# A hybrid attention and recurrent block: x loaded transposed, the norm applied to the products of ten weight chunks, h rescaled in place later

## The chip, the cores and the metric

One core of one Trainium2 chip runs the kernel. The metric is the device time of one execution in microseconds, the median of three runs. The engines are PE (matrix products), DVE (vector), ACT (activations, table functions), POOL (a second, general vector engine) and SP, which issues most of the DMAs.

## What is computed

One layer of a decoder block on x of 1024 tokens by 1024 features, float32. Cut to what the change is about:

```python
def rms_norm(x, g):
    y = x * rsqrt(mean(x * x, -1) + EPS)
    return y * g

h = rms_norm(x, norm_gain)
proj = h @ w_in
q, kv_all, g_nsa, br_gate, u_lru, g_lru, merge_g = split(proj)
y_a = nsa_mixer(q, kv_all, br_gate, ...)   # compressed, selected and window attention
y_a = (y_a * silu(g_nsa)) @ w_proj_a
y_b = rglru_mixer(u_lru, conv_w, ...)      # causal convolution, two gates, a scan over the tokens
y_b = (y_b * silu(g_lru)) @ w_proj_b
m = sigmoid(gate_a) * y_a + sigmoid(gate_b) * y_b
x = x + m @ w_out
```

There are 8 query heads of 64 in two groups with keys and values of their own, and the recurrent mixer is 512 wide.

## The kernel before

Tokens and features both lie in blocks of 128, and the tokens in two halves of 512. Each large product is made of float32 operands that are split in a high and a low part: `mm3` issues high by high (line 170), high by low (171) and low by high (172), so that all large products have these three lines. Weights are split as they come (`wsplit`, line 182 and on): the high part on ACT (line 184), the low part on POOL or DVE (line 185). h itself is needed transposed, features on partitions: `hT_h` (the tile is named big_h) and `hT_l` (big_l, one tile for each half).

**Head** (lines 195 to 239). x comes by eight token blocks of 512 KB (lines 217, 221), in between the first two weight chunks (`wload`, line 176) and the small parameters. For each block ACT squares and sums (line 228), POOL takes the power -1/2 (lines 192, 193), DVE multiplies the block by it (line 231). PE transposes each half by 32 blocks of 128x128 (line 235), four into a bank of PSUM; ACT copies the bank times the gain (line 237) and DVE makes the low part of it (line 238).

**Chunks.** `chunk(c)` (line 259) multiplies 128 columns of w_in with h: 24 products for each half of the tokens, in a bank of its own. Five banks take turns (`ps_5`: four named ps_s, one ps_f). Chunks 0 to 7 are u and the gate of the four parts of the recurrent mixer (`lru(n)`, line 321): ACT copies u out of the banks (line 325), DVE makes the convolution (330, 333), ACT and DVE split the result (336, 337), the silu of the gate is a sigmoid on ACT (343) and a product with the bank on DVE (344). After two small products ACT makes the two gates; DVE follows with lines 361, 362 (a RECIPROCAL of 128x1024), 363, 364, 366 and the scan 367, with POOL's products at 365 and 368. Chunks 8 and 9 are the compressed keys and values (`compress`, line 372). These parts are generators, and the string ORD, "0c1c0c2c1c323", says in which order they are taken a step further.

**q, k, v.** `qkv(g)` (line 469) projects q, the keys, values and branch gates for one group, with tokens on partitions, from block 7 down to block 0: 48 products of 262 columns into two banks for each block, copied by ACT (498, 499) and for the gates by DVE (500). Blocks 7 to 4 read the second half of h, 3 to 0 the first. For group 0 each block goes through `prep` at once: squares on ACT (531), sums (533), power on POOL (192, 193), products on DVE (536) and POOL (537, 538), split on ACT and DVE (541 to 546) and POOL (550), transposes (554, 561) and copies (556, 565). For group 1 the projection runs beside the scores of group 0. The tile named t has nine buffers, and st four.

The order on each engine is fixed when the program is built: a scheduler places the instructions by priorities and by durations of its own, and each engine then runs its list in order, waiting on semaphores.

Of the kernel before, what the change touches and what calls it, by code (L numbers as in the profile page):

```python
# [9 lines left out]
FT = mybir.dt.float32  # L10
# [16 lines left out]
SMALL = (("gain", 8), ("kgain", 192), ("qgain", 64), ("w4", 128), ("lru_p", 32), ("cb1", 4), ("pe", 32))  # L27
# [10 lines left out]
SO = (1, 1)  # L38
# [15 lines left out]
XW = 5  # L54
# [32 lines left out]
def _build(ctx, tc, A, out, dbg):  # L87
# [58 lines left out]
    # after the attention: banks and blocks that it held  # L146
# [32 lines left out]
    def wsplit(raw, k, into=None, E=None):  # L179
        """hi and lo parts of 1024 weights per partition, as [128, k, n]"""  # L180
# [18 lines left out]
    make_identity(nc, ident)  # L199
    G.tensor_copy(ident_r, ident)  # L200
    ident = f(ident_r)
    small = K.tile([128, NSMALL], FT, name="small")
    part = {}
# [4 lines left out]
    gain = part["gain"]  # L208
# [10 lines left out]
    dma(small, A["small"])  # L219
    for tb in range(4, 8):  # L220
        dma(xt[tb], A["x"][tb * 128:(tb + 1) * 128, :])
        if tb == XW:
            first.append(wload(A["w_in"][1]))
    for half in range(2):
        xs = xt[half * 4:half * 4 + 4]
        for b in range(4):
            tb = half * 4 + b
            C.activation(junk[:, (b % 2) * S:(b % 2 + 1) * S], xs[b], AF.Square, scale=DM ** -0.5,
                         accum_out=ssq[:, tb:tb + 1])
            rsq(rstd[:, tb:tb + 1], ssq[:, tb:tb + 1], EPS, 128, 1)  # L230
# [22 lines left out]
    def chunk_half(o, wh, wl, half):  # L253
        """o [128, 512] = w^T h^T, tokens of one half"""
# [4 lines left out]
    def chunk(c):  # L259
        E = EN[(CE >> c) & 1]  # L260
        wh, wl = wsplit(first.pop(0), 8, None, E) if first else wtile(A["w_in"][c], 8, None, E)
        s = []
# [36 lines left out]
    # -4 softplus(-lambda): log1p by the series of atanh  # L299
# [19 lines left out]
    yb = DR.tile([4, 128, S], FT, name="yb")  # L319

    def lru(n):
        s = chunk(2 * n)
# [15 lines left out]
        s = chunk(2 * n + 1)  # L338
# [15 lines left out]
        # t = tanh(log_a / 2): a = (1 + t) / (1 - t), sqrt(1 - a^2) = 2 sqrt(-t) / (1 - t)  # L354
# [18 lines left out]
    def compress():  # L373
        big, dup = p_slc(), p_win()
        kv = [big[:, j * S:(j + 1) * S] for j in range(2)]
        for j in range(2):
            s = chunk(8 + j)
            for half in range(2):
                C.activation(kv[j][:, half * 512:(half + 1) * 512], s[half], AF.Copy)
        yield  # L380
        for j in range(2):
# [3 lines left out]
            for g in range(2):  # L385
# [3 lines left out]
                for b in range(2):  # L389
                    # token 16 (c + b) + 2 l  # L390
# [716 lines left out]
```

## Time and profile before

| quantity | value |
|---|---|
| median of the runs (lowest, highest) | 909.04 us (908.88, 909.33) |
| profiled execution: span, device time | 908.0 us, 909.0 us |
| PE busy | 874.2 us, 96% of the span |
| DVE, ACT, POOL busy | 573.3, 439.1, 300.6 us |
| first product of a chunk on PE | at 15.81 us |
| first scores | at 239.90 us |

Times in the trace are microseconds from the start of the span. The busy time of an engine contains what an instruction stands still once it has begun; idle time is shown with the event that ended it. A busy PE is not always at its full clock: the granted clock stands in the windows.

### The profile page before, as it was taken

Reading aid. Unit: us, or ns where it says so; the run is one execution under the profiler, and the core shown is the slowest. Engines: PE = TensorE matmul, PEld = TensorE weight load, DVE = VectorE, ACT = ScalarE, POOL = GpSimd, SP = SyncE. Lnnn points to the kernel's source line nnn. Section 1 sums busy time; section 2 is a strip of 40 time slices with the busy share of each in tenths; the row PEclk is TensorE's granted clock in tenths of the full one; section 3 lists DMA queues with packets and bytes.
Section 4 is the critical chain, followed back from the end, with each engine's and each line's share of the span. In section 5 each row is a group of like instructions: output and inputs, shape, how many; then the busy total and the mean of one; then the engine's idle time right before and its main releaser. Section 6 shows DMA issues by size and latency. Waiting matters only on the chain.

```text
span 908.0 us, 15833 instructions
## 1 busy us (share of the span) xinstructions
PE 874.2 (96%) x5670; PEld 781.0 (86%) x5670; DVE 573.3 (63%) x1626; ACT 439.1 (48%) x1159; POOL 300.6 (33%) x339
## 2 busy tenths in 40 slices
PE   4999999989899999999999999999999899999998
PEld 3678878889899999999999998999999877888887
DVE  5642778897722447475687867677777886784111
ACT  6421434645523548575566666566667663321000
POOL 4122233169622325252455553243233421000000
PEclk9999999999999999999999999999999999999999
DMA  9215321121312112122121232111113469983111
GB/s 340 64 49 139 131 95 55 55 82 48 117 48 82 59 48 74 52 86 69 55 66 65 77 102 75 47 54 60 46 42 119 132 202 331 336 270 119 70 70 47
DMA packets 45519, 92.49 MB, mean 102 GB/s; under 512 B 6896, under 2 KB 12704, under 8 KB 45440
## 3 DMA queue, kind: packets, MB, share of 16 engines
q1 hardware_dynamic: 44480, 88.33, 28.9%
q0 software_dynamic: 960, 3.15, 0.9%
q8 instruction: 44, 0.72, 0.3%
q14 instruction: 35, 0.29, 0.1%
HBM read 64.15 MB, written 25.21 MB: 98 GB/s over the span
## 4 chain that ended last, share of the span: by engine, by line
PE 80%; DVE 7%; DMA 4%; POOL 4%; issue 2%; ACT 2%; SPq 0%; DVEq 0%; ACTq 0%; POOLq 0%
PE ps_f L170 9%; PE ps_f L171 9%; PE ps_f L172 9%; PE ps_s L612 7%; PE ps_s L170 7%; PE ps_s L171 7%; PE ps_s L172 7%; PE ps_t L665 6%; PE ps_t L170 4%; PE ps_t L171 4%; PE ps_t L172 4%; PE ps_o L690 3%; PE ps_o L689 3%; POOL ss L193 1%; DVE sq L536 1%
## 5 line engine op out<-in xcount | busy, mean ns | idle before, releaser
L171 PE MATMUL ps_f<-big_l,w_hi 128*128 128x256 f32 (+1 forms) x700 | 200.3, 286 | 0.0
L170 PE MATMUL ps_f<-big_h,w_hi 128*128 128x256 f32 (+1 forms) x664 | 193.8, 292 | 1.0 <-ACT ev L829 0.8
L172 PE MATMUL ps_f<-big_h,w_lo 128*128 128x256 f32 (+1 forms) x664 | 189.4, 285 | 0.0
L171 PEld LDWEIGHTS ps_f<-big_l,w_hi 128*128 128x128 f32 x700 | 131.9, 188 | 2.1
L170 PEld LDWEIGHTS ps_f<-big_h,w_hi 128*128 128x128 f32 x664 | 125.6, 189 | 4.1 <-ACT ev L829 2.3
L172 PEld LDWEIGHTS ps_f<-big_h,w_lo 128*128 128x128 f32 x664 | 125.4, 189 | 1.6
L670 DVE TENSOR_TENSOR pl<-ps_t,ph 128x512 fp32r<-128x512 f32 x132 | 90.4, 686 | 47.5 <-ACT ph L669 46.0
L185 POOL TENSOR_TENSOR w_lo<-w_raw,w_hi 128x1024 fp32r<-128x1024 f32 x33 | 80.7, 2448 | 102.1 <-ACT w_hi L184 101.7
L669 ACT ACTIVATE ph<-ps_t 128x512 fp32r<-128x512 f32 x132 | 78.1, 599 | 48.8 <-PE ps_t L665 45.6
L650 POOL TENSOR_SCALAR p_slc<-p_slc,mx,bg 128x384 f32<-128x384 f32 (+7 forms) x88 | 68.7, 786 | 89.5 <-DVE mx L649 34.8
L646 ACT ACTIVATE p_slc<-ps_s,mx 128x256 f32<-128x256 f32 (+5 forms) x128 | 68.1, 541 | 24.1 <-DVE mx L644 18.6
L171 PE MATMUL ps_s<-big_l,w_hi 128*128 128x512 f32 (+1 forms) x184 | 73.8, 401 | 0.0
L184 ACT ACTIVATE w_hi<-w_raw 128x1024 fp32r<-128x1024 f32 (+1 forms) x40 | 42.4, 1062 | 43.6 <-PE ps_f L171 17.5
L636 DVE TENSOR_REDUCE mx<-ps_s 128x1 f32<-128x256 f32 (+5 forms) x120 | 50.9, 436 | 11.0 <-PE ps_s L612 9.3
L170 PE MATMUL ps_s<-big_h,w_hi 128*128 128x512 f32 x136 | 55.3, 408 | 2.5 <-ACT big_h L237 2.5
L689 PE MATMUL ps_o<-ph,t 128*128 128x512 f32 x132 | 55.7, 422 | 0.0
L650 POOL TENSOR_SCALAR p_win<-p_win,mx,bg 128x640 f32<-128x640 f32 (+1 forms) x40 | 34.7, 869 | 59.3 <-DVE mx L649 25.5
L665 PE MATMUL ps_t<-ident_r,p_slc 128*128 128x128 f32 x336 | 54.2, 273 | 0.0
L612 PE MATMUL ps_s<-kTs,t 128*128 128x512 f32 (+4 forms) x224 | 53.0, 349 | 0.6 <-ACT pc L621 0.3
L172 PE MATMUL ps_s<-big_h,w_lo 128*128 128x512 f32 x136 | 53.5, 397 | 0.0
L641 DVE CUSTOM_DVE_ANT_0 ps_s<-ps_s,bias 128x256 f32<-128x256 f32 (+1 forms) x128 | 52.5, 417 | 1.4 <-PE ps_s L612 0.3
L690 PE MATMUL ps_o<-pl,t 128*128 128x512 f32 x132 | 53.2, 403 | 0.0
(331 smaller groups left out, 2213.3 us busy)
## 6 DMA issues: line engine op xcount, KB each, us to landing
w_raw<-in_w_in SPq DMA_DIRECT2D x30, 512.0 KB
t<-in_x SPq DMA_DIRECT2D x8, 512.0 KB
gb<-ev SPq DMA_DIRECT2D x16, 256.0 KB
ga<-ev SPq DMA_DIRECT2D x16, 256.0 KB
w_raw<-in_w_out SPq DMA_DIRECT2D x8, 512.0 KB
st<-mb SPq DMA_DIRECT2D x16, 256.0 KB
w_raw<-in_w_tok SPq DMA_DIRECT2D x6, 524.0 KB
ev<-in_cw SPq DMA_DIRECT2D x8, 256.0 KB
```

Of the source, the lines that this page charges most:

```text
L170: T.matmul(o, lh, rh, start=first, stop=False)
L171: T.matmul(o, lh, rl, start=False, stop=False)
L172: T.matmul(o, ll, rh, start=False, stop=last)
L185: (E or (V if tail else G)).tensor_tensor(out=lo, in0=raw, in1=f(hi), op=OP.subtract)
L612: T.matmul(s, qT[h][:, i * 128:(i + 1) * 128], rhs, start=(hl == 0), stop=(hl == 1))
L646: C.activation(p[:, h, k0:k1], sv, AF.Exp, bias=mx[:, 6:7], accum_out=mx[:, 7 + j:8 + j])
L650: G.tensor_scalar(out=p[:, h], in0=p[:, h], scalar1=mx[:, 9:10], scalar2=bg[:, g, i, 4 * (br + 1) + h:4 * (br + 1) + h + 1], op0=OP.mult, ...
L665: ins = T.transpose(pt[:, h * 128:(h + 1) * 128], p[h][:, c0:c0 + 128], ident)
L669: C.activation(ph, pt, AF.Copy)
L670: V.tensor_tensor(out=pl, in0=pt, in1=f(ph), op=OP.subtract)
L689: T.matmul(o, vf, pp[0], start=first, stop=False)
L690: T.matmul(o, vf, pp[1], start=False, stop=False)
```

## The change

- x comes in a second, transposed layout as well: eight tiles of 512 KB, features on partitions, four for each half of the tokens; the first one as two DMAs. The first weights come right behind it, the second behind the first half of x, the small parameters behind all of x, and the gain by a DMA of its own on ACT's queue.
- `split_x` makes h without the norm: gain times x on ACT, its low part on DVE. No transposes, no norm ahead of the products.
- `norms` makes the squares (ACT), their sums over tiles (DVE for the first half, POOL for the second), eight products of one column with ones that sum over partitions, the power on POOL, a diagonal on DVE, and one product of ones and the diagonal, which puts the norm of each token on all partitions: R, one tile of 128x512 for each half, in two of the four buffers of st.
- `chunks` takes two chunks together: both weights are held, the first half of the tokens for both, then the second. u, the gate and the compressed keys and values are multiplied by R as DVE reads them out of PSUM; the last product of the silu goes to POOL.
- `rescale(half)` turns h into the normed h in place: four times the sum of both parts on POOL, its product with R on DVE, the high part on ACT, the low part on DVE, each 128x1024. In the code the first half stands ahead of block 7 of group 0, the second ahead of block 3. Blocks 7 to 4 of group 0 still read the h without norm and are multiplied at the copy out of PSUM.

The core of the diff (lines with comments alone and the constants that are no longer used are left out):

```diff
-    xt = [ta() for _ in range(NT)]
-    for tb in range(4):
-        dma(xt[tb], A["x"][tb * 128:(tb + 1) * 128, :])
-    first = [wload(A["w_in"][0])]
...
-            rsq(rstd[:, tb:tb + 1], ssq[:, tb:tb + 1], EPS, 128, 1)
-            V.tensor_scalar(out=xs[b], in0=xs[b], scalar1=rstd[:, tb:tb + 1], scalar2=None, op0=OP.mult)
-        for kc in range(8):
-            pt = (ps_t, ps_t, ps_o)[SO[half] and kc % 3]()
-            for b in range(4):
-                T.transpose(pt[:, b * 128:(b + 1) * 128], xs[b][:, kc * 128:(kc + 1) * 128], ident)
...
+    R = [t_st() for _ in range(2)]
+    def split_x(half):
+        for j in range(4):
+            for k in range(2):
+                kc = 2 * j + k
+                hh = hT_h[:, kc, half * 512:(half + 1) * 512]
+                C.activation(hh, xt[half][j][:, k], AF.Copy, scale=gain[:, kc:kc + 1])
+                V.scalar_tensor_tensor(out=hT_l[half][:, kc], in0=xt[half][j][:, k],
+                                       scalar=gain[:, kc:kc + 1], in1=f(hh), op0=OP.mult, op1=OP.subtract)
+    def norms(half):
+        acc = junk[:, half * S:(half + 1) * S].rearrange("p (k n) -> p k n", k=2)
+        C.activation(acc, xt[half][0], AF.Square, scale=DM ** -0.5)
+        for j in range(1, 4):
+            C.activation(xt[half][j], xt[half][j], AF.Square, scale=DM ** -0.5)
+            (V, G)[half].tensor_tensor(out=acc, in0=acc, in1=xt[half][j], op=OP.add)
...
+                T.matmul(o[:, b:b + 1], acc[:, k, b * 128:(b + 1) * 128], ones[:, 0:1], start=(k == 0), stop=(k == 1))
...
+        T.matmul(o, ones, dg, start=True, stop=True)
+        V.tensor_copy(R[half], o)
+    split_x(0)
+    pending = [lambda: norms(0), lambda: split_x(1), lambda: norms(1)]
+    def rescale(half):
+        for j in range(4):
+            t = ta().rearrange("p (k n) -> p k n", k=2)
+            hh = hT_h[:, 2 * j:2 * j + 2, half * 512:(half + 1) * 512]
+            ll = hT_l[half][:, 2 * j:2 * j + 2]
+            G.tensor_tensor(out=t, in0=f(hh), in1=f(ll), op=OP.add)
+            V.tensor_tensor(out=t, in0=t, in1=R[half][:, None, :].to_broadcast([128, 2, 512]), op=OP.mult)
+            C.activation(hh, t, AF.Copy)
+            V.tensor_tensor(out=ll, in0=t, in1=f(hh), op=OP.subtract)
...
+        for half in range(2):
+            for k, (wh, wl) in enumerate(ws):
+                s[k][half] = ps_5()
+                chunk_half(s[k][half], wh, wl, half)
...
-            C.activation(u[:, half * 512:(half + 1) * 512], s[half], AF.Copy)
+            V.tensor_tensor(out=u[:, half * 512:(half + 1) * 512], in0=s[half], in1=R[half], op=OP.mult)
...
-            C.activation(sg[:, t], s[half], AF.Sigmoid)
-            V.tensor_tensor(out=sg[:, t], in0=sg[:, t], in1=s[half], op=OP.mult)
+            V.tensor_tensor(out=i[:, t], in0=sz[half], in1=R[half], op=OP.mult)
+            C.activation(sg[:, t], i[:, t], AF.Sigmoid)
+            G.tensor_tensor(out=sg[:, t], in0=sg[:, t], in1=i[:, t], op=OP.mult)
...
+        if not g:
+            rescale(0)
         for tb in range(NT - 1, -1, -1):
+            if not g and tb == 3:
+                rescale(1)
...
+                r = rstd[:, tb:tb + 1] if not g and tb > 3 else 1.0
+                C.activation(e[:, 0:262], o[0][:, 0:262], AF.Copy, scale=r)
+                C.activation(e[:, 262:512], o[1][:, 0:250], AF.Copy, scale=r)
+                V.tensor_scalar(out=bg[:, g, tb], in0=o[1][:, 250:262], scalar1=r, scalar2=None, op0=OP.mult)
```

Three places of the order that the prediction speaks of. In the changed kernel the lines of `mm3` are 168 to 170, 268 to 274 are `rescale`, and big_l_100 and big_l_101 are the low parts of the first and of the second half of h.

PE, the head, before: L235 are the transposes of x, L170 to L172 the products of the first chunk.

```order
L235 MATMUL ps_o<-ident_r,t 128x128
L235 MATMUL ps_t<-ident_r,t 128x128 [waits DVE_49]
L235 MATMUL ps_t<-ident_r,t 128x128
L235 MATMUL ps_o<-ident_r,t 128x128
L170 MATMUL ps_s<-big_h,w_hi 128x512 [waits Activation_49]
L235 MATMUL ps_t<-ident_r,t 128x128 [waits DVE_49]
L235 MATMUL ps_t<-ident_r,t 128x128 x3
L171 MATMUL ps_s<-big_l_75,w_hi 128x512
L172 MATMUL ps_s<-big_h,w_lo 128x512 [waits Pool_49]
L170 MATMUL ps_s<-big_h,w_hi 128x512 [waits Activation_49]
```

And now, from the first instruction on:

```order
L168 MATMUL ps_s<-big_h,w_hi 128x512 [waits Activation_49]
L169 MATMUL ps_s<-big_l_100,w_hi 128x512 [waits DVE_49]
L170 MATMUL ps_s<-big_h,w_lo 128x512 [waits DVE_49]
L168 MATMUL ps_s<-big_h,w_hi 128x512
L169 MATMUL ps_s<-big_l_100,w_hi 128x512
L170 MATMUL ps_s<-big_h,w_lo 128x512
```

The transposes are gone; the products wait for ACT's and DVE's parts of x alone.

DVE, between the branch gates of the first blocks of q, k, v and the last part of the recurrent mixer, before: L362, L363, L364, L366 and L367 are the mixer's RECIPROCAL, products and scan, L455 and L460 copies of a bias, L533 and L536 steps of `prep`.

```order
L362 RECIPROCAL t<-t 128x1024 [waits DVE_49]
L367 SCALAR_TENSOR_TENSOR t<-t,kTs 128x1024 [waits DVE_49]
L455 COPY bias<-t 128x1024 [waits DMAHW1_49,PE_49]
L536 TENSOR_TENSOR sq<-ev,ss 128x384 [waits Pool_49]
L455 COPY bias<-t 128x1024 [waits DMAHW2_49]
L500 COPY bg<-ps_s 128x12 [waits Activation_49]
L533 TENSOR_REDUCE ss<-sq 128x6 [waits Activation_49]
L460 COPY cbias<-t 128x512 [waits DMAHW4_49,DMAHW5_49,DMAHW3_49,DMAHW6_49,DMAHW2_49,DMAHW7_49,DMAHW1_49,DMAHW0_49]
L500 COPY bg<-ps_f 128x12 [waits Activation_49]
L363 SCALAR_TENSOR_TENSOR t<-t 128x1024 [waits DVE_49]
L364 SCALAR_TENSOR_TENSOR t<-t 128x1024
L344 TENSOR_TENSOR kTs<-kTs,ps_s 128x512 [waits Activation_49] x2
```

And now, at the place behind the same RECIPROCAL; L406, L407 and L410 are two products and the scan of the mixer, L272 and L274 the product and the subtraction of `rescale`, L580 to L593 steps of `prep`.

```order
L406 SCALAR_TENSOR_TENSOR t<-t 128x1024 [waits DVE_49]
L407 SCALAR_TENSOR_TENSOR t<-t 128x1024
L410 SCALAR_TENSOR_TENSOR t<-t,kTs 128x1024 [waits DVE_49]
L272 TENSOR_TENSOR t<-t,st 128x1024 [waits Pool_49]
L589 TENSOR_TENSOR st<-sq,st 128x4x64 [waits Activation_49]
L593 TENSOR_TENSOR st<-sq,st 128x2x128 [waits Activation_49]
L272 TENSOR_TENSOR t<-t,st 128x1024 [waits Pool_49] x2
L274 TENSOR_TENSOR big_l_100<-t,big_h 128x1024 [waits Activation_49]
L580 TENSOR_REDUCE ss<-sq 128x6 [waits Activation_49]
L272 TENSOR_TENSOR t<-t,st 128x1024 [waits Pool_49]
L274 TENSOR_TENSOR big_l_100<-t,big_h 128x1024 [waits Activation_49]
L583 TENSOR_TENSOR sq<-ev,ss 128x384 [waits Pool_49]
```

The rescaling stands behind the scan, and in between the preparation of the first blocks; each L272 waits for POOL's sum.

PE, the end of the fourth and the start of the fifth block of q, k, v (the first that reads the first half of h), before; p_slc and w_hi, w_lo hold the weights' parts:

```order
L171 MATMUL ps_s<-p_slc,big_h 128x262
L172 MATMUL ps_s<-p_slc,big_l_76 128x262
L170 MATMUL ps_f<-w_hi,big_h 128x262 [waits DVE_49]
L171 MATMUL ps_f<-w_lo,big_h 128x262
L172 MATMUL ps_f<-w_hi,big_l_75 128x262
```

And now:

```order
L169 MATMUL ps_s<-p_slc,big_h 128x262
L170 MATMUL ps_s<-p_slc,big_l_101 128x262
L168 MATMUL ps_f<-w_hi,big_h 128x262 [waits Activation_49]
L169 MATMUL ps_f<-w_lo,big_h 128x262
L170 MATMUL ps_f<-w_hi,big_l_100 128x262 [waits DVE_49]
```

Before, the block waited for a bank alone; now its products wait for ACT's and DVE's parts of the rescaled h.

## Rows read from the trace of the kernel before

**Rows 1.** The page: span; busy time of each engine, its share, instructions.
```profile
span 908.0 us, 15833 instructions
...
PE 874.2 (96%) x5670; PEld 781.0 (86%) x5670; DVE 573.3 (63%) x1626; ACT 439.1 (48%) x1159; POOL 300.6 (33%) x339
```

**Rows 2.** Windows: length; busy us (instructions) by engine; TensorE clock; DMA share; GB/s.
```profile
10.00:20.00 10.00, 6.00 (x20) 4.27 (x21) 8.70 (x21) 6.55 (x13) 5.46 (x8) 1.00 1.03 385
...
96.00:168.00 72.00, 71.45 (x383) 59.14 (x381) 56.04 (x43) 32.07 (x47) 22.30 (x12) 1.00 0.27 91
...
177.30:239.90 62.60, 55.81 (x441) 54.27 (x439) 55.32 (x76) 32.15 (x89) 48.59 (x52) 0.97 0.23 73
```

**Rows 3.** Waits of PE, 0 to 300 us: total us, times, longest us.
```profile
PE ps_t L235 <- DVE t L231: 9.7, 4, 7.3
...
PE ps_s L612 <- ACT t L565: 2.4, 1, 2.4
```

**Rows 4.** Timeline of PE, first 40 us: start, length, engine, line, operation [idle before].
```profile
15.81 0.80 PE L170 MATMUL ps_s<-big_h,w_hi 128*128 128x512 f32 x1 [2.50 <-ACT big_h L237]
...
31.92 0.47 PE L170 MATMUL ps_s<-big_h,w_hi 128*128 128x512 f32 x1
32.24 0.40 PE L171 MATMUL ps_s<-big_l,w_hi 128*128 128x512 f32 x1
32.47 0.39 PE L172 MATMUL ps_s<-big_h,w_lo 128*128 128x512 f32 x1
...
35.25 0.60 PE L235 MATMUL ps_t<-ident_r,t 128*128 128x128 f32 x4
35.60 0.48 PE L171 MATMUL ps_s<-big_l,w_hi 128*128 128x512 f32 x1
...
37.38 1.02 PE L280 MATMUL ps_o<-t,rel 32*8 32x512 f32 x2
38.33 0.50 PE L170 MATMUL ps_s<-big_h,w_hi 128*128 128x512 f32 x1
```

**Rows 5.** Timeline of ACT, first 12 us.
```profile
4.33 1.06 ACT L228 ACTIVATE p_win<-t 128x1024 f32<-128x1024 f32 x1 [2.31 <-DMA t<-in_x]
...
8.03 1.06 ACT L228 ACTIVATE p_win<-t 128x1024 f32<-128x1024 f32 x1 [1.31 <-DMA t<-in_x]
...
10.54 1.06 ACT L184 ACTIVATE w_hi<-w_raw 128x1024 fp32r<-128x1024 f32 x1
```

**Rows 6.** Lines of DVE by form, 168 to 240 us: busy us, mean ns.
```profile
L344 DVE TENSOR_TENSOR kTs<-kTs,ps_s 128x512 f32<-128x512 f32 x2 | 1.3, 674 | 0.0
```

**Rows 7.** Timeline of DVE, 168 to 240 us.
```profile
177.36 2.70 DVE L363 SCALAR_TENSOR_TENSOR t<-t 128x1024 f32<-128x1024 f32 x1
179.98 1.22 DVE L364 SCALAR_TENSOR_TENSOR t<-t 128x1024 f32<-128x1024 f32 x1
...
183.39 6.54 DVE L362 RECIPROCAL t<-t 128x1024 f32<-128x1024 f32 x1
...
201.09 2.54 DVE L542 TENSOR_TENSOR st<-sq,st 128x256 fp32r<-128x256 f32 x1
...
220.81 0.43 DVE L542 TENSOR_TENSOR st<-sq,st 128x256 fp32r<-128x256 f32 x1 [0.94 <-ACT st L541]
```

**Rows 8.** Timeline of POOL, 168 to 240 us.
```profile
176.54 2.44 POOL L365 TENSOR_TENSOR kTs<-kTs,t 128x1024 f32<-128x1024 f32 x1 [19.34 <-ACT kTs L352]
...
200.94 2.41 POOL L365 TENSOR_TENSOR kTs<-kTs,t 128x1024 f32<-128x1024 f32 x1
...
220.71 1.32 POOL L193 TENSOR_TENSOR ss<-ss,nhalf 128x6 f32<-128x6 f32 x1
```

**Rows 9.** Timeline of PE, 190 to 202 us.
```profile
196.15 0.39 PE L170 MATMUL ps_s<-w_hi,big_h 128*128 128x262 f32 x1 [2.80 <-DVE bg L500]
...
197.41 0.42 PE L170 MATMUL ps_s<-w_hi,big_h 128*128 128x262 f32 x1
...
200.68 0.30 PE L170 MATMUL ps_f<-w_hi,big_h 128*128 128x262 f32 x1
```

More of the change, by code (lines that the diff above doesn't have):

```diff
@@ L26 @@
 NB = 71
-SMALL = (("gain", 8), ("kgain", 192), ("qgain", 64), ("w4", 128), ("lru_p", 32), ("cb1", 4), ("pe", 32))
+SMALL = (("kgain", 192), ("qgain", 64), ("w4", 128), ("lru_p", 32), ("cb1", 4), ("pe", 32))
 NSMALL = sum(w for _, w in SMALL)
@@ L53 @@
 NPL = 3
-XW = 5
 PF = 1
@@ L198, in _build @@
     ident = junk[:, 2 * S:2 * S + 128]
-    make_identity(nc, ident)
-    G.tensor_copy(ident_r, ident)
-    ident = f(ident_r)
+    ones = junk[:, 2 * S + 128:2 * S + 256]
+    gain = K.tile([128, 8], FT, name="gain")
+    nc.scalar.dma_start(gain, A["gain"])
+    xt = [[ta().rearrange("p (k n) -> p k n", k=2) for _ in range(4)] for _ in range(2)]
+    first = []
+    for half in range(2):
+        for j in range(4):
+            if (half, j) == (0, 0):
+                for k in range(2):
+                    dma(xt[0][0][:, k], A["xT"][0, 0, :, k])
+                first.append(wload(A["w_in"][0]))
+            else:
+                dma(xt[half][j], A["xT"][half, j])
+            if (half, j) == (0, 3):
+                first.append(wload(A["w_in"][1]))
     small = K.tile([128, NSMALL], FT, name="small")
+    dma(small, A["small"])
     part = {}
@@ L207, in _build @@
         c0 += w
-    gain = part["gain"]
+    make_identity(nc, ident)
+    G.tensor_copy(ident_r, ident)
+    ident = f(ident_r)
+    V.memset(ones, 1.0)
     hT_h = K.tile([128, 8, S], FR, name="big_h")
@@ new lines, in _build @@
+    R = [t_st() for _ in range(2)]
+    def split_x(half):
+        for j in range(4):
+            for k in range(2):
+                kc = 2 * j + k
[9 more added lines that the diff above has]
+            (V, G)[half].tensor_tensor(out=acc, in0=acc, in1=xt[half][j], op=OP.add)
+        o = ps_t()
+        h4 = slice(half * 4, half * 4 + 4)
+        for b in range(4):
+            for k in range(2):
+                T.matmul(o[:, b:b + 1], acc[:, k, b * 128:(b + 1) * 128], ones[:, 0:1], start=(k == 0), stop=(k == 1))
+        V.tensor_scalar(out=ssq[:, h4], in0=o[:, 0:4], scalar1=1.0, scalar2=EPS, op0=OP.mult, op1=OP.add)
+        G.tensor_tensor(out=rstd[:, h4], in0=ssq[:, h4], in1=nhalf[:, 0:4], op=OP.pow)
+        dg = acc[:, 0]
+        for b in range(4):
+            V.tensor_scalar(out=dg[:, b * 128:(b + 1) * 128], in0=ident, scalar1=rstd[:, half * 4 + b:half * 4 + b + 1],
+                            scalar2=None, op0=OP.mult)
+        o = ps_t()
+        T.matmul(o, ones, dg, start=True, stop=True)
+        V.tensor_copy(R[half], o)
@@ new lines, in _build @@
+    split_x(0)
+    pending = [lambda: norms(0), lambda: split_x(1), lambda: norms(1)]
+    def rescale(half):
+        for j in range(4):
+            t = ta().rearrange("p (k n) -> p k n", k=2)
[5 more added lines that the diff above has]
+            V.tensor_tensor(out=ll, in0=t, in1=f(hh), op=OP.subtract)
@@ L257, in chunk_half, with chunks @@
             mm3(o, wh[:, kc], wl[:, kc], hT_h[:, kc, t], hT_l[half][:, kc], kc == 0, kc == 7)
[L259 to L262, printed above, removed]
-        for half in range(2):
-            s.append(ps_5())
-            chunk_half(s[half], wh, wl, half)
+    def chunks(*cs):
+        ws = []
+        for c in cs:
+            E = V if first else EN[(CE >> c) & 1]
+            ws.append(wsplit(first.pop(0), 8, None, E) if first else wtile(A["w_in"][c], 8, None, E))
+        s = [[None, None] for _ in cs]
+        for half in range(2):
+            for k, (wh, wl) in enumerate(ws):
+                s[k][half] = ps_5()
+                chunk_half(s[k][half], wh, wl, half)
+                if pending:
+                    pending.pop(0)()
+            while pending and not half:
+                pending.pop(0)()
         return s
@@ L375, in compress @@
         kv = [big[:, j * S:(j + 1) * S] for j in range(2)]
-        for j in range(2):
-            s = chunk(8 + j)
+        for j, s in enumerate(chunks(8, 9)):
             for half in range(2):
-                C.activation(kv[j][:, half * 512:(half + 1) * 512], s[half], AF.Copy)
+                V.tensor_tensor(out=kv[j][:, half * 512:(half + 1) * 512], in0=s[half], in1=R[half], op=OP.mult)
         yield
```

22 lines of the change are left out of this document (2 added, 20 removed).

## The prediction

> **What bounds the kernel now.** I read the page first. PE is busy for 874.2 of 908.0 us [rows 1], so wherever PE works without a gap only a smaller amount of PE work helps, and wherever it has a gap the view of waits says whose fault that is. The windows show three different stages. In the head, 10 to 20 us, PE has 6.00 us of work in 10 while DVE has 8.70 [rows 2]: PE waits there for the normalised x, 9.7 us in all, ahead of its transposes [rows 3], and its first product starts at 15.81 [rows 4]. From 96 to 168 us PE is busy for 71.45 of 72 us and DVE for 56.04 [rows 2]; PE decides, but DVE has only 22% to give. From 177.30 to 239.90, which is the projection of q, k and v for group 0 up to the first scores, PE is busy for 55.81 of 62.60 us, DVE for 55.32 and POOL for 48.59 [rows 2]. That is the one early stage in which three engines are nearly full, and PE's gaps there are DVE's and ACT's fault: 2.80 us before a block of q, k, v whose bank is not yet free [rows 9], 2.4 us before the first scores [rows 3]. The change takes work out of the first stage and puts it into the second and the third.
>
> The third stage has a second feature, seen when the timelines of DVE and POOL are laid side by side. A DVE product of two SBUF tiles of 128x1024 takes 1.22 us at 179.98 [rows 7]; the same kind of instruction takes 2.70 when it starts at 177.36, inside a POOL product that runs from 176.54 for 2.44 [rows 7, 8]. A 128x256 product takes 0.43 at 220.81 and 2.54 at 201.09, where POOL has begun a 2.41 product at 200.94 [rows 7, 8]. So two such instructions, one on each engine, do not run side by side here: the second stands still, though shown as busy, until the first is done. The RECIPROCAL (one input) starts at 183.39 with its 6.54 us [rows 7] and is not affected. DVE's 55.32 busy us therefore contain its standing behind POOL already.
>
> **The change, part by part.** The sum is made against this execution: span 908.0, device time 909.0 with 1.0 outside of the span, which is also the median of the runs (909.04).
>
> *Head.* The 64 transposes go, and so does the norm ahead of the products. How far is PE ahead? Before, the product at 31.92 is the 26th [rows 4]: 25 products at the dense pitch of 0.23 (32.24 to 32.47) put the start of an unbroken series at 31.92 - 5.75 = 26.2, and the 16 transposes still to come at 0.35 for four (35.25 to 35.60) make it 27.6. After, the first x tile comes as two DMAs of 256 KB and the weights as the next one. The first 512 KB of x were there at 4.33 and the third at 8.03 [rows 5], so I estimate the first quarter megabyte at 3.6 and the weights near 6. ACT then has two casts of 512 columns (about 0.6 each, half of a 1.06 and a start), a square (1.06) and the split of the weights (1.06) [rows 5] in order: the first product starts at about 8.1. Then ACT issues six more casts, two squares and the second split, and DVE, which takes the low parts of x and of both weights, ends the second low part near 17.1; 28 products are done by then, so the unbroken series begins at 17.1 - 28 x 0.23 = 10.7. PE gets new work: two 128x512 products for the broadcast of the norm, at 0.95 (37.38 to 38.33, one fp32 product recorded as two) [rows 4], and 16 products of one column, which no row shows. They are bounded by nothing but an issue, 0.06, and by the pitch of a 512-column product, 0.23; I take 0.17, as fp32 ones are recorded as two. Together 1.9 + 2.7 = 4.6. Lead of PE: 27.6 - 10.7 - 4.6 = 12.3 us, 10 if ACT's chain of casts and squares for the second half holds the products up by 2. The DMA of the gain on ACT's queue and the later place of the small parameters on SP's cost nothing: x and weights are ahead of them in what PE waits for.
>
> *LRU stage.* Twelve evacuations (eight of u, four of k and v) move from ACT to DVE as products of a bank and R. The nearest row is the silu product of a bank and a tile, 0.674 [rows 6], so 12 x 0.67 = 8.1, and 1.3 for the two copies of R. The z evacuation replaces that silu product one for one. If all 9.4 lie on the path, 12.3 shrinks to 2.9; if all are hidden, it stays at 12.3. I take 5, nearer to the lower end: DVE is 78% busy there and its row of convolution, RECIPROCAL and scan now starts only when both chunks of a pair are done, since the chunks run in pairs, half by half.
>
> *q, k, v of group 0.* This is where the change is paid for. Each half is rescaled in four steps of 128x1024: an add of the two parts on POOL (nearest row 2.41, a product of the same size [rows 8]), a multiplication and a subtraction on DVE (1.22 each [rows 7]), a cast on ACT (1.06 [rows 5]). All three of POOL's and DVE's have two SBUF inputs and so take turns: 8 x (2.41 + 2 x 1.22) = 38.8. The last silu's two products move to POOL as well, 2 x 1.2 = 2.4. Together 41.2 that DVE either does or stands behind; ACT's 8.5 lie beside it, since ACT is busy for only 32.15 [rows 2]. What hides it: one add goes under the RECIPROCAL of 6.54, -2.4 (the second waits for a tile that is freed after it); DVE's idle time is 62.60 - 55.32 = 7.3, of which I count half, -3.6, since the rest are round trips of a block's norm between ACT, DVE and POOL; and the lead, -5. PE waits first at the fifth block (200.68 before [rows 9]), which reads the first rescaled half, then at the first block for group 1, which reads the second; the blocks of the preparation that the scores need stand in the same DVE and POOL order and come late with it. After a wait as long as this PE runs slowly: behind the 2.80 us one, products go at a pitch of 0.13 up to 197.41 and then 15 of them at 0.22 up to 200.68 [rows 9], the lower level of 1.2 GHz, so +1.5.
>
> Sum: -5 + 41.2 - 2.4 - 3.6 + 1.5 = +31.7, 909.0 + 31.7 = 940.7. With no lead, no idle time used and no add hidden it is +42.7, about 952; with the lead whole, all idle time used and two adds hidden it is 41.2 - 12.3 - 7.3 - 4.8 + 1.5 = +18, about 927.
>
> *A rule against a row.* POOL's power for the norm of a head (1.32 at 220.71) and a DVE product (0.43 at 220.81) did run side by side [rows 7, 8], so I do not count the eight powers of this stage among what takes turns. The Trainium skill (SBUF — State Buffer, "Who interferes with whom") says that a DVE instruction with two SBUF inputs contends with any GpSimd instruction that reads SBUF, which the power does. By that rule DVE would find no idle time to give, and the sum would be 3.6 higher, 944.3.
>
> **The rivals.** *Not exclusive.* The long DVE rows might be late inputs and not POOL's doing. Then only DVE's own share counts, 8 x 2 x 1.22 = 19.5, less its idle 7.3 and the lead of 5: +7, about 916 (909 to 922). For it: POOL has 14 us free in the stage. Against it: both inflated rows end about one own length after POOL's (177.36 + 2.70 = 180.06 against 176.54 + 2.44 + 1.22 = 180.20).
>
> *The rescale fits (other side).* The place is the fifth block. The first half of h is free once the last pair of chunks has passed to its second half, 48 products or 11 us before q, k, v begin, and four blocks of 48 products for the other half of the tokens, 25 us at 0.13 each, lie between that and the first read. If POOL and DVE start on it then, at once, its 19.4 us are done within 36, PE keeps its lead and the second half is done within the next 25. It decides if the rescale's first product on DVE starts before the third block does. Then PE gets 12.3 less 1.3 for the copies of R, all of it: 909.0 - 11 = 898 (896 to 907). For it: PE is the bound for most of the program, and time gained ahead is kept unless a wait takes it. Against it: the order puts the first rescaling product on DVE behind the scan that follows the RECIPROCAL, and that RECIPROCAL ended at 189.93 [rows 7], 11 us before the fifth block; and 41 us do not go into what DVE has free, 7.3.
>
> **How the numbers follow.** The main case has 0.76 (its own range 925 to 953), the two rivals 0.12 each. The low end reaches to 909 to take in the case in which the engines do not take turns; the high end is the main one with nothing hidden: 909 to 953. Faster is the case in which the rescale fits, 0.12; within 0.2% (1.8 us, about what a measurement of this kernel can tell) is the edge of the middle one, 0.03; the rest is slower, 0.85.
>
> **What would show it.** Right: no transposes in the head and a first product near 8 us; PE waiting for 8 us or more ahead of the fifth block, released by the rescale's subtraction or cast; a second wait ahead of the first block of group 1 or the first scores; rescaling products on DVE at 2.4 us and more beside POOL's adds; the first scores near 270 instead of 239.90. Wrong: adds and DVE products overlapping at their own lengths, or PE reaching the fifth block without a wait, with its time from then on ahead of the old one.

## The result and the profile after

The changed kernel takes 954.25 us (median of four runs, 953.05 to 957.81) against 909.06: a ratio of 1.050, 95% interval 1.048 to 1.052. It is slower, as forecast, but by 45 us and not by 31.7, and 1 us above the upper end of the range. The profiled execution took 953.3 us, 951.6 of it in the span. In the changed kernel the lines of `mm3` are 168 to 170.

The page of the changed kernel answers to [rows 1]:

```profile
span 951.6 us, 15809 instructions
...
PE 887.8 (93%) x5642; PEld 792.9 (83%) x5642; DVE 625.3 (66%) x1664; ACT 441.7 (46%) x1147; POOL 340.1 (36%) x342
```

All engines have more to do, but PE only 13.6 us more (887.8 against 874.2), while the span is 43.6 longer. The rest is waiting. The view of PE's waits of the changed kernel, whole run, its first five rows (total us, times, longest):

```profile
PE ps_s L168 <- ACT w_hi L182: 8.5, 1, 8.5
PE ps_t L461 <- DVE t L456: 8.2, 2, 4.2
PE ps_f L168 <- ACT big_h L273: 8.1, 1, 8.1
PE ps_f L170 <- DVE big_l L274: 5.6, 2, 4.5
PE ps_s L168 <- ACT big_h L273: 5.2, 2, 3.5
```

The transposes' waits of [rows 3] are gone. In their place PE waits 8.5 for its first weights, twice for some 4 us ahead of line 461 (the second layer of the compression), and 18.9 us in the three last rows for the rescaled h. The timeline of PE, changed kernel, shows where:

```profile
8.50 0.80 PE L168 MATMUL ps_s<-big_h,w_hi 128*128 128x512 f32 x1 [8.50 <-ACT w_hi L182]
...
26.04 1.95 PE L251 MATMUL ps_t<-p_win 128*128 128x1 f32 x16
...
29.45 0.63 PE L168 MATMUL ps_s<-big_h,w_hi 128*128 128x512 f32 x1
29.87 0.63 PE L169 MATMUL ps_s<-big_l,w_hi 128*128 128x512 f32 x1
...
111.28 0.48 PE L461 MATMUL ps_t<-t 128*64 128x64 f32 x2 [4.23 <-DVE t L456]
...
152.36 0.47 PE L461 MATMUL ps_t<-t 128*64 128x64 f32 x2 [3.99 <-DVE t L456]
...
217.09 0.58 PE L168 MATMUL ps_f<-w_hi,big_h 128*128 128x262 f32 x1 [8.11 <-ACT big_h L273]
...
272.06 0.95 PE L659 MATMUL ps_s<-t 128*128 128x384 f32 x3
```

The first product starts at 8.50 instead of 15.81. At 26.04 eight of the sixteen products of one column stand, recorded as sixteen; products behind them go at a pitch (start to start) of 0.42 (29.45 to 29.87), not 0.23. Then the waits at 111.28 and 152.36, the wait ahead of the fifth block at 217.09 (200.68 before), and the first scores at 272.06 (239.90 before). The windows of the changed kernel (columns as in [rows 2]) say the same by stage: PE had no wait from 96 to 168 us before, and now loses 4 of 20 us in two windows, with the granted clock down to 0.83 in both; from 177.30 on it is busy for 44.80 us where it was for 55.81, and DVE is still full.

```profile
100.00:120.00 20.00, 15.77 (x68) 12.29 (x67) 17.36 (x13) 3.02 (x8) 3.08 (x4) 0.83 0.37 128
140.00:160.00 20.00, 16.01 (x72) 12.73 (x71) 16.27 (x11) 8.86 (x10) 5.26 (x2) 0.83 0.03 8
177.30:239.90 62.60, 44.80 (x305) 42.92 (x304) 56.77 (x45) 28.64 (x54) 44.34 (x31) 0.81 0.13 39
```

To see at which point the time goes, count PE's products: 480 of 128x512 with h in the ten chunks, then 768 of 262 columns for q, k, v. The table gives the start of the 97th chunk product, of the first q, k, v product, of the 193rd (the fifth block) and of the 529th, read off PE's timelines, as differences to the kernel before (53.62, 167.88, 200.68 and 254.92 us); it has a row for each run of the study. The four differences come from the one profiled execution of each kernel, the median from all its runs; the profiled execution of "single, no rescale" took 909.7 us, 3.8 more than its median.

| kernel | median us | 97th | first of q, k, v | fifth block | 529th |
|---|---|---|---|---|---|
| the change | 954.25 | -7.5 | +7.7 | +16.4 | +43.0 |
| no rescale | 921.7 | -6.8 | +7.9 | +3.4 | +9.5 |
| single chunks | 938.1 | -7.0 | -5.8 | +2.7 | +25.9 |
| adds on DVE | 946.6 | -4.4 | +8.8 | +17.3 | +35.0 |
| x loaded again | 942.8 | -5.9 | +6.9 | +10.2 | +30.1 |
| u by ACT | 948.5 | -8.6 | +0.5 | +11.5 | +37.0 |
| single, x loaded again | 928.1 | -5.3 | -3.8 | +0.4 | +18.3 |
| single, no rescale | 905.9 | -3.7 | -2.4 | -2.8 | -2.0 |
| before, with pairs | 914.7 | -4.8 | +8.1 | +3.0 | +4.0 |
| wide ones | 948.0 | -10.7 | +3.9 | +12.6 | +36.8 |
| norm first, 1st try | 913.5 | +5.2 | +6.5 | +6.2 | +4.9 |
| norm first, 2nd try | 906.5 | -7.0 | -2.4 | -2.6 | -4.1 |

So the changed kernel is 7.5 us ahead after the head, 7.7 behind when q, k, v begin, and 43.0 behind when the rescale is over; after that it loses only 0.6 more. One gain and two losses, one in each stage, and the experiments take them one by one. The first column is the least certain: the kernels with the same head and with pairs are between 4.4 and 8.6 us ahead there.

### The profile page after: what moved, and what is told of

Same layout as the page of the kernel before. It is cut to its first block, busy times and chain, and to the rows that moved or that the text cites. A ratio compares the mean times of both kernels' runs of the same rounds, so it can differ in the third digit from the quotient of the medians.

```text
span 951.6 us, 15809 instructions
## 1 busy us (share of the span) xinstructions
PE 887.8 (93%) x5642; PEld 792.9 (83%) x5642; DVE 625.3 (66%) x1664; ACT 441.7 (46%) x1147; POOL 340.1 (36%) x342
## 4 chain that ended last, share of the span: by engine, by line
PE 76%; DVE 13%; DMA 4%; ACT 4%; issue 2%; POOL 1%; SPq 0%; DVEq 0%; ACTq 0%; POOLq 0%
PE ps_f L168 9%; PE ps_f L169 9%; PE ps_f L170 9%; PE ps_s L659 7%; PE ps_s L168 6%; PE ps_s L169 6%; PE ps_s L170 6%; PE ps_t L712 5%; PE ps_t L168 3%; PE ps_t L170 3%; PE ps_t L169 3%; PE ps_o L737 3%; PE ps_o L736 3%; DVE t L272 2%; DVE t L405 1%
## 5 line engine op out<-in xcount | busy, mean ns | idle before, releaser
L170 PE MATMUL ps_f<-big_h,w_lo 128*128 128x256 f32 (+1 forms) x664 | 189.6, 285 | 0.0
L170 PEld LDWEIGHTS ps_f<-big_h,w_lo 128*128 128x128 f32 x664 | 125.4, 189 | 1.6
L183 POOL TENSOR_TENSOR w_lo<-w_raw,w_hi 128x1024 fp32r<-128x1024 f32 x31 | 78.5, 2535 | 73.4 <-ACT w_hi L182 73.0
L169 PE MATMUL ps_s<-big_l,w_hi 128*128 128x512 f32 (+1 forms) x184 | 76.6, 416 | 0.0
L168 PE MATMUL ps_s<-big_h,w_hi 128*128 128x512 f32 x136 | 59.3, 437 | 8.5 <-ACT w_hi L182 8.5
L170 PE MATMUL ps_s<-big_h,w_lo 128*128 128x512 f32 x136 | 57.5, 424 | 0.0
```

The costliest lines, as they stand in the source:

```text
L168: T.matmul(o, lh, rh, start=first, stop=False)
L169: T.matmul(o, lh, rl, start=False, stop=False)
L170: T.matmul(o, ll, rh, start=False, stop=last)
L183: (E or (V if tail else G)).tensor_tensor(out=lo, in0=raw, in1=f(hi), op=OP.subtract)
```

## The experiments

**The rescale left out.**

```diff
-        if not g:
-            rescale(0)
...
-            if not g and tb == 3:
-                rescale(1)
...
-                r = rstd[:, tb:tb + 1] if not g and tb > 3 else 1.0
+                r = rstd[:, tb:tb + 1]
```

> Leaves out: the rescale of h; q, k, v of both groups are multiplied by the norm as they leave PSUM, the 20 gate chunks stay without the norm. Theory A (the rescale costs 36 us by the turns that POOL and DVE take, the other 8 or 9 us of the loss come from the LRU stage, where PE falls 8 us behind): 915 to 922 us, and the first q, k, v product still some 7 us later than in the kernel before. Rival B (PE's lag at the start of q, k, v is harmless, all of the loss is the rescale): 905 to 911. Rival C (the rescale is a small part): above 935.

Measured: 921.7 us, ratio 1.0129 (1.0111 to 1.0148). The rescale is worth 32.6 of the 45 us, and the time lies within the range of theory A. The lag of 7.9 us at the first product of q, k, v is still there. It shrinks to 3.4 at the fifth block, but is 9.5 at the 529th: PE waits behind the fifth block for DVE's copies of line 599 (3.3 and 2.1 us in all, ahead of lines 597 and 604). The pairing alone in the kernel before (below) does not show that second loss (3.0, then 4.0), so its cause stays open.

**The adds on DVE.**

```diff
-            G.tensor_tensor(out=t, in0=f(hh), in1=f(ll), op=OP.add)
+            V.tensor_tensor(out=t, in0=f(hh), in1=f(ll), op=OP.add)
```

> The eight adds of the rescale on DVE instead of POOL. Theory A (a POOL add stops DVE for its 2.41 us, the same add on DVE takes 1.22): faster by 8 x 1.2, 941 to 949 us. Rival (the two engines work side by side, DVE's own work is what counts): slower by 8 x 1.22, 960 to 966.

Measured: 946.6 us, ratio 1.0405 (1.0385 to 1.0425). DVE got eight instructions more, 12 us of work, and the kernel became 7.7 us faster, as theory A had it. The lines by form, first DVE in the changed kernel, then POOL in it, then DVE with the adds (190 to 292 us; busy us, mean ns; idle time behind the second bar):

```profile
L272 DVE TENSOR_TENSOR t<-t,st 128x1024 f32<-128x1024 f32 x8 | 16.7, 2093 | 0.0
...
L274 DVE TENSOR_TENSOR big_l<-t,big_h 128x1024 fp32r<-128x1024 f32 x8 | 10.2, 1276 | 0.7 <-ACT big_h L273 0.7
```

```profile
L271 POOL TENSOR_TENSOR t<-big_h,big_l 128x1024 f32<-128x1024 f32 x8 | 22.1, 2766 | 8.6 <-DVE bias L497 5.9 <-DVE big_l L274 1.3 <-DVE t L407 1.2
```

```profile
L271 DVE TENSOR_TENSOR t<-big_h,big_l 128x1024 f32<-128x1024 f32 x8 | 12.2, 1533 | 0.0
...
L272 DVE TENSOR_TENSOR t<-t,st 128x1024 f32<-128x1024 f32 x8 | 10.2, 1287 | 0.0
```

With the adds on POOL (22.1 us) the multiplications take 16.7 us; with the adds on DVE (12.2 us) the same multiplications take 10.2. Only some 2 of these 6.5 us were spent behind an add (212.65 in DVE's timeline, shown in the next section); the others stood behind other POOL work. The adds stop other lines of DVE as well. Laid beside DVE's timeline, each of the eight has a DVE instruction that starts inside it and does not end before it: two copies, line 407, one multiplication, and four steps of `prep`, of which this is one (DVE, then POOL, changed kernel):

```profile
261.10 2.74 DVE L583 TENSOR_TENSOR sq<-ev,ss 128x384 f32<-128x384 f32 x1
```

```profile
261.04 2.37 POOL L271 TENSOR_TENSOR t<-big_h,big_l 128x1024 f32<-128x1024 f32 x1
```

Line 583 takes 0.55 to 0.67 us when it meets nothing (198.19, 225.08). From the start of each of the eight to the end of its add are 1.7 to 2.3 us, 16.9 in all: POOL's adds run in the stead of DVE's work and not beside it, and on DVE itself they take 12.2. Each step of the rescale, an add, a product, a cast and a subtraction in a row, is also 1.2 us shorter by it (1533 against 2766 ns for the add), which works the same way; the run does not separate the two.

**x loaded again instead of added up.**

```diff
-            G.tensor_tensor(out=t, in0=f(hh), in1=f(ll), op=OP.add)
-            V.tensor_tensor(out=t, in0=t, in1=R[half][:, None, :].to_broadcast([128, 2, 512]), op=OP.mult)
+            dma(t, A["xT"][half, j])
+            for k in range(2):
+                V.scalar_tensor_tensor(out=t[:, k], in0=t[:, k], scalar=gain[:, 2 * j + k:2 * j + k + 1],
+                                       in1=R[half], op0=OP.mult, op1=OP.mult)
```

> The rescale takes x once more from memory (eight DMAs of 512 KB) and makes x times gain times R in one pass on DVE, instead of adding the two parts on POOL and multiplying on DVE. DVE's work is the same. Theory A (DVE stands behind POOL's adds, 8 x 2.41 = 19 us): 933 to 941 us. Rival (the adds run beside DVE): 951 to 957. Rival (the reload waits for a free buffer or the DMA): above 957.

Measured: 942.8 us, ratio 1.0372 (1.0347 to 1.0397): 11.5 us faster, and 1.8 above the range of theory A. The adds are off the path, but DVE's own passes stay, about 20 us by themselves (16 of 1.22), and PE still loses 23.2 us from the first product of q, k, v to the 529th.

**Chunks one at a time.**

```diff
-        s, sz = chunks(2 * n, 2 * n + 1)
+        s, = chunks(2 * n)
...
+        sz, = chunks(2 * n + 1)
...
-        for j, s in enumerate(chunks(8, 9)):
+        for j in range(2):
+            s, = chunks(8 + j)
```

> Chunks one at a time, as before the change, all else of the change kept. Theory A (the pairing puts the products of an LRU part behind both chunks of its pair, and so the RECIPROCAL and with it the compression's small products come late; this loses the head's lead): 938 to 946 us, no waits of 4 us ahead of the compression's second layer. Rival B (the twelve evacuations that moved to DVE lose it; the pairing matters little): 950 to 957, the waits stay.

Measured: 938.1 us, ratio 1.0314 (1.0286 to 1.0341). All twelve evacuations are still on DVE, and the lead of the head comes through the LRU stage nearly whole (-7.0 to -5.8): theory A. Of the waits ahead of the compression's second layer 0.5 us are left, as in the kernel before (view of PE's waits, 60 to 176 us):

```profile
PE ps_t L463 <- DVE t L458: 0.5, 1, 0.5
```

**The pairing alone, in the kernel before.**

```diff
-        s = chunk(2 * n)
+        s, sz = chunks(2 * n, 2 * n + 1)
...
-        s = chunk(2 * n + 1)
+        s = sz
```

> The kernel before with one part of the change alone: chunks in pairs, each half of the tokens for both. Theory A (the pairing by itself makes the LRU stage late, whoever empties the banks): the compression's second layer waits for DVE behind a RECIPROCAL, 913 to 920 us. Rival B (the pairing only hurts with the evacuations on DVE): 907 to 911.

(`chunks` is the function of the change; the compressed keys and values are paired by it as well.) Measured: 914.7 us, ratio 1.0069 (1.0055 to 1.0082), in the range of theory A. ACT empties the banks here, DVE has no evacuation of u, and the wait appears all the same (same view and stretch):

```profile
PE ps_t L421 <- DVE t L416: 5.7, 1, 5.7
```

From the 97th product to the first of q, k, v PE loses 12.9 us in this kernel and 15.2 in the changed one: the pairing is most of that loss. The whole becomes only about 6 us longer: of the 8.1 us that PE is late at the first of q, k, v, 3.0 are left at the fifth block.

**u, keys and values by ACT, pairs kept.**

```diff
-            V.tensor_tensor(out=u[:, half * 512:(half + 1) * 512], in0=s[half], in1=R[half], op=OP.mult)
+            C.activation(u[:, half * 512:(half + 1) * 512], s[half], AF.Copy)
```

> Leaves out: the norm of u and of the compressed keys and values; ACT copies them out of PSUM as in the kernel before, so that DVE loses twelve products of 0.67 us. The pairing stays. Theory A (the pairing makes the LRU stage late): 949 to 956 us, the two waits of 4 us ahead of the compression's second layer stay. Rival B (DVE's twelve evacuations make it late): 938 to 946, the waits shrink.

(The compressed keys and values likewise.) Measured: 948.5 us, ratio 1.0436 (1.0416 to 1.0457), half a microsecond below the range of theory A and 2.5 above that of B. One of the two waits is gone, the other grew:

```profile
PE ps_t L461 <- DVE t L456: 5.7, 1, 5.7
```

The twelve evacuations cost some 6 us, which is less than the 8.1 of work in them, and they cost that only with pairs: with single chunks they lay hidden.

**Both at once.** Single chunks, and the rescale from x loaded again (both edits as above).

> Chunks one at a time and the rescale from x loaded once more. Theory A (the two losses lie in stages that follow each other and add up): the pairing's 16 and the adds' 11 us go together, 924 to 930 us. Rival (the time that one frees is lost by the other, since both are DVE's): 934 to 938.

Measured: 928.1 us, ratio 1.0201 (1.0186 to 1.0216). The two gains, 16.1 and 11.5, make 27.6 together; 26.1 came. They lie in stages that follow each other.

**Single chunks without the rescale** (both edits as above).

> Leaves out: the rescale, so that the 20 gate chunks stay without the norm (q, k, v get it as they leave PSUM). Chunks one at a time. Theory A (the head's gain of some 6 us is real and kept once neither pairing nor rescale takes it): 902 to 907 us. Rival (the evacuations on DVE eat it anyway): 909 or above.

Measured: 905.9 us, ratio 0.9961 (0.9947 to 0.9975). It is in the range of theory A. The head's gain is real, and about 3 us of it are left at the end in a kernel that leaves out what takes it.

**Wide ones.**

```diff
-                T.matmul(o[:, b:b + 1], acc[:, k, b * 128:(b + 1) * 128], ones[:, 0:1], start=(k == 0), stop=(k == 1))
+                T.matmul(o[:, b * 128:(b + 1) * 128], acc[:, k, b * 128:(b + 1) * 128], ones, start=(k == 0), stop=(k == 1))
```

> The changed kernel with the sixteen products of one column made 128 columns wide. Theory A (PE's clock falls after them because they hardly use it): the products behind them keep the pitch of 0.23, and at the 97th chunk product PE is some 11 us ahead of the kernel before instead of 7.5; the whole hardly moves, 950 to 955, since the wait for DVE in the LRU stage ends when DVE does. Rival (the clock falls for another reason): the pitch of 0.43 stays and the lead at that product too.

Measured: 948.0 us, ratio 1.0434 (1.0420 to 1.0449). The pitch behind them is 0.23 (PE's timeline, 28.91 to 29.14), and PE is 10.7 us ahead at the 97th product:

```profile
25.62 2.05 PE L251 MATMUL ps_t<-p_win 128*128 128x128 f32 x16
...
28.91 0.39 PE L169 MATMUL ps_s<-big_l,w_hi 128*128 128x512 f32 x1
29.14 0.40 PE L170 MATMUL ps_s<-big_h,w_lo 128*128 128x512 f32 x1
```

The second part of the expectation fell: the whole became 6 us faster. The waits ahead of line 461 are as long as before (4.2 and 4.0), only earlier. DVE's RECIPROCAL there begins at 98.75 instead of 101.92, earlier by as much as PE is, so what PE gains in the head moves both, and is not swallowed: 3.8 us of it are there at the first product of q, k, v. Why the rescale then costs another 2.4 less was not looked into. That narrow products alone lower the clock is not settled by this run (see the last section).

**Another head: the norm first.** It asks whether the transposed x can be had without what it cost. In the kernel before, the head alone is replaced: squares in fp32r, summed over partitions by products with ones of 128 columns, root on ACT, reciprocal on DVE, and h with its norm from the start.

```diff
+    def norm(half):
+        o = ps_t()
+        for j in range(4):
+            sq = pre[:, (j % 2) * S:(j % 2 + 1) * S].rearrange("p (k n) -> p k n", k=2)
+            C.activation(sq, xt[half][j], AF.Square, scale=DM ** -0.5)
+            for k in range(2):
+                T.matmul(o, ones, sq[:, k], start=(j + k == 0), stop=(j + k == 4))
+        R = t_st()
+        C.activation(R, o, AF.Sqrt, bias=eps_t)
+        V.reciprocal(R, R)
+        return R
+    def split_h(half, R):
+        for kc in range(8):
+            xs = xt[half][kc // 2][:, kc % 2]
+            tn = te2(("ep", "eo")[kc % 2])
+            V.scalar_tensor_tensor(out=tn, in0=xs, scalar=gain[:, kc:kc + 1], in1=R, op0=OP.mult, op1=OP.mult)
...
-        s = chunk(2 * n)
+        s, sz = chunks(0, 1) if n == 0 else (chunk(2 * n), None)
```

The first try made the norm of the second half behind the split of the first, the second try during it, with the small parameters and the bias rows loaded later. The cut above is of the second try.

> The kernel before with another head: x transposed in memory, its squares summed over partitions by products with ones (fp32r), the root on ACT and the reciprocal on DVE, then x times gain times norm on DVE, split as before; only the first two chunks are paired, no rescale, no evacuation by R. Theory (the transposes and DVE's late norm cost the head some 6 us that nothing else needs): first product near 15 us, 902 to 907 us. Rival (DVE and ACT cannot make the second half of h by the time PE has done the first, PE waits 5 us or more there): 909 to 915.

> The other head again, with the norm of the second half made while the first half is split, and the small parameters and the bias rows loaded behind it. Theory (its loss was the second half's norm, for which PE stood still from 34 to 41 us and then ran slowly): no such wait, 901 to 907 us. Rival (DVE's passes over x, 1.4 us for each of 16 slices, set the pace anyway): 908 to 913.

Measured: 913.5 us, ratio 1.0038 (1.0024 to 1.0052) for the first, 906.5, ratio 0.9975 (0.9965 to 0.9986) for the second. The first missed its theory and came out in the rival's range: its first product started at 19.34, not near 15, and PE stood still ahead of 39.62 for a product of the bias rows that DVE made behind the norm of the second half (its PE timeline). The second came out within its theory; PE's longest wait behind the first product of its head is 0.89 us (its PE timeline, at 42.24):

```profile
19.34 1.22 PE L170 MATMUL ps_s<-big_h,w_hi 128*128 128x512 f32 x2 [7.76 <-ACT big_h L244]
...
39.62 1.87 PE L304 MATMUL ps_o<-t,rel 32*8 32x512 f32 x2 [4.28 <-DVE t L305]
```

```profile
18.07 1.05 PE L170 MATMUL ps_s<-big_h,w_hi 128*128 128x512 f32 x2
...
42.24 0.49 PE L171 MATMUL ps_s<-big_l,w_hi 128*128 128x512 f32 x1 [0.89 <-DVE big_l L248]
```

So a version that beats both kernels exists: it drops the transposes and adds no pass over h to the later stages. What it gains is 2 us.

## Why the prediction was wrong, and where it was right

**The head: right in kind, too high by some 5 us.** First product 8.50 (8.1 forecast). The lead was forecast at 12.3, or 10 at the least; it was 7.5 at the 97th product. 3.2 of the difference are the slow products behind those of one column; the wide ones give them back. The products of one column, which the step had priced by their own length alone, 0.17 each or 2.7 together, took some 3.7 (the first eight 1.81 to the next product, 0.23 each, which was the upper of its two bounds). And PE waited 1.2 us ahead of 39.66 for a bias row from DVE. These three make 5.4; what gave back the rest was not taken apart.

**The LRU stage: the step that failed.** The text took "I take 5" from bounds of 2.9 and 12.3. Measured, PE was 7.7 behind when q, k, v began, and the RECIPROCAL that had ended at 189.93 ended at 197.73: outside of both bounds, 12.7 away from the lead of 5 in the sum. Of these, 4.8 came with the smaller lead of the head; 7.9 are this step's own, since the stage took 15.2 us of PE's lead and not 12.3 - 5 = 7.3, and more than the 9.4 that were meant as its most. 940.7 + 12.7 is 953.4, and that this meets the measured time so closely is luck in part: the rescale came out 1.4 below its forecast, and the rest of the program about as much above. The bounds added up work (twelve evacuations, two copies) and asked how much of it DVE could hide. The loss came from the order. DVE, changed kernel, 100 to 230 us:

```profile
101.92 6.52 DVE L405 RECIPROCAL t<-t 128x1024 f32<-128x1024 f32 x1
108.37 2.68 DVE L434 TENSOR_TENSOR p_slc<-p_win,small 128x504 f32<-128x504 f32 x3
110.90 0.59 DVE L456 SCALAR_TENSOR_TENSOR t<-ps_s,small,t 128x128 f32<-128x128 f32 x2
...
191.18 6.55 DVE L405 RECIPROCAL t<-t 128x1024 f32<-128x1024 f32 x1
197.64 0.63 DVE L497 COPY bias<-t 128x1024 f32<-128x1024 f32 x1
...
198.65 2.86 DVE L497 COPY bias<-t 128x1024 f32<-128x1024 f32 x1
...
207.15 3.38 DVE L407 SCALAR_TENSOR_TENSOR t<-t 128x1024 f32<-128x1024 f32 x1
...
212.65 3.29 DVE L272 TENSOR_TENSOR t<-t,st 128x1024 f32<-128x1024 f32 x1
...
228.01 1.26 DVE L274 TENSOR_TENSOR big_l<-t,big_h 128x1024 fp32r<-128x1024 f32 x1
```

Line 456, which frees PE's wait of 4.23 at 111.28, stands behind the RECIPROCAL of 101.92 and three adds. Before, the same line (414, and PE's line is 419) stood behind a RECIPROCAL as well; DVE's and PE's timelines of the kernel before:

```profile
102.51 6.55 DVE L362 RECIPROCAL t<-t 128x1024 f32<-128x1024 f32 x1
```

```profile
114.50 0.33 PE L419 MATMUL ps_t<-t 128*64 128x64 f32 x2 [0.54 <-DVE t L414]
```

PE now comes to this place at 107.05 instead of 113.96, 6.9 us earlier, but the RECIPROCAL begins only 0.6 earlier: DVE's row has not followed PE's lead. With chunks in pairs u is whole after 72 products of a pair and not after 48, 24 x 0.23 = 5.5 us later against PE's own row, and the work on DVE that hangs on u moves with it; with single chunks the same RECIPROCAL begins at 96.06, 5.9 earlier (DVE's timeline of that run). The wait is 4.0 to 5.7 in all kernels with pairs in this stage and 0.5 in those without. Behind each wait PE runs slowly: the granted clock of both windows is 0.83, and some thirteen products go at 0.43 instead of 0.23, 2.6 us more. Twice 4.1 and 2.6 are 13.4 of the 15.2. That the row would start later stood in the text; that something of PE's hung behind it, and what, did not.

**The rescale: right in kind and in size, though not in each term.** From the first product of q, k, v to the 529th PE loses 35.3 us (43.0 - 7.7). The forecast for the stage, without the lead, was 41.2 - 2.4 - 3.6 + 1.5 = 36.7. The 2.4 for an add under the RECIPROCAL did not come: the first add began at 198.35, after the RECIPROCAL had ended at 197.73. So the sum is better than its parts. That POOL's adds and DVE's work take turns is seen at all eight adds, and the adds moved to DVE and x loaded again bear out its price. The rival "not exclusive" falls: by it the adds on DVE would have made the kernel slower (960 to 966 expected, 946.6 measured). POOL's timeline in the changed kernel shows three of the adds, beside DVE's lines above:

```profile
198.35 2.61 POOL L271 TENSOR_TENSOR t<-big_h,big_l 128x1024 f32<-128x1024 f32 x1 [5.91 <-DVE bias L497]
...
206.23 3.21 POOL L271 TENSOR_TENSOR t<-big_h,big_l 128x1024 f32<-128x1024 f32 x1
210.67 4.19 POOL L271 TENSOR_TENSOR t<-big_h,big_l 128x1024 f32<-128x1024 f32 x1 [1.23 <-DVE t L407]
...
228.15 2.31 POOL L191 TENSOR_TENSOR ss<-ss,nhalf 128x6 f32<-128x6 f32 x1
```

The add at 206.23 covers DVE's line 407 at 207.15, which took 3.38 instead of 1.22; the add at 210.67 in turn took 4.19, since DVE had begun a scan before it. PE waited first at the fifth block and then for the second half, as forecast.

**The rival on the other side fell** by its own condition: the first rescaling product on DVE came at 212.65, after the third block (190.09 in the changed kernel), and PE waited 8.11 at the fifth.

## What to carry to other kernels

A lead that is won at the front is worth what the last wait behind it leaves of it: follow it through each stage, and price the order, not the work. When two pieces of PE's work are interleaved so that the first one's result comes later, list what hangs on this result on the other engines, and what of PE's hangs on that in turn. Work for two engines that cannot run side by side is to be added up as on one.

## What the runs showed of the hardware

Sixteen fp32 records of one column and sixteen of 128 columns take about the same time (1.95 and 2.05 us), with PE busy without a gap before, in and behind both. Behind the narrow ones the granted clock falls to the lower level of 1.2 GHz in most runs, and behind the wide ones it did not. Windows of the changed kernel, then of the one with wide ones, then the narrow ones and the windows of "single, no rescale":

```profile
26.00:28.00 2.00, 2.00 (x18) 1.96 (x18) 2.00 (x2) 1.06 (x1) 2.00 (x1) 1.00 1.00 239
28.00:30.00 2.00, 2.00 (x7) 1.58 (x8) 1.83 (x8) 0.07 (x1) 0.45 (x1) 0.67 0.65 200
30.00:32.00 2.00, 2.00 (x6) 1.19 (x4) 1.76 (x10) 0.99 (x1) 1.50 (x2) 0.50 0.11 27
```

```profile
28.00:30.00 2.00, 2.00 (x10) 1.49 (x8) 1.80 (x10) 0.29 (x1) 0.15 (x1) 1.00 0.47 156
30.00:32.00 2.00, 2.00 (x8) 0.85 (x7) 1.79 (x9) 0.76 (x1) 1.80 (x2) 1.00 0.09 22
```

```profile
24.87 1.95 PE L251 MATMUL ps_t<-p_win 128*128 128x1 f32 x16
```

```profile
26.00:28.00 2.00, 2.00 (x14) 1.77 (x14) 2.00 (x2) 1.06 (x1) 2.00 (x1) 1.00 1.24 210
28.00:30.00 2.00, 2.00 (x9) 0.96 (x7) 1.83 (x8) 0.68 (x1) 0.35 (x1) 1.00 0.43 147
```

In this last kernel, and in the one with the adds on DVE, the clock stays up behind the same sixteen records and the pitch stays at 0.23. Of the eight kernels with narrow products six slow down behind the first eight of them, and seven behind the second eight, ahead of which PE had also waited for 1.2 us or more. So the narrow products alone do not decide it, and two groups of wide ones are few: that their width is the cause is likely and not shown.

A copy of 128x1024 with one input stands still beside a POOL add as well: 2.86 us at 198.65, beside the add of 198.35, where its twin of 197.64 took 0.63. The prediction had counted only instructions with two inputs as taking turns. The Trainium skill (SBUF — State Buffer, "Who interferes with whom") names copies among those that can take the shared ports; the trace agrees.

In these traces POOL's power waits only when it starts: 2.31 us at 228.15, just behind the start of DVE's line 274 (228.01, 1.26), against 1.32 us when it came first and a DVE product ran inside it [rows 7, 8]. In the kernel with the adds on DVE even a product of 128x1024 kept its length, 1.21 us at 220.92, inside a power that began at 220.76 and took 1.32. By the same section of the Trainium skill, which says it of DVE's modes with two ports, whichever instruction comes first has the shared ports for its whole length; the runs show that for adds, and not for the power.
